# Two-layer decoder on one core: where the low parts of layer 0's weights are computed

## The chip, the core and the metric

The kernel runs on one core of one Trainium2 chip. A core has TensorE (PE, the matrix engine), VectorE (DVE), ScalarE (ACT), GpSimd (POOL) and SyncE (SP, which here only issues transfers). The metric is the device time of one execution in microseconds (us); the figure of a kernel is the median of its runs.

## The reference, cut to what matters

Two post-norm decoder layers over 512 tokens of width 1024, in float32. Layer 0 has two head groups, differential attention (4 heads) and a sparse attention (8 query heads in 2 groups, each with a compressed, a selected and a window branch); layer 1 has a forgetting attention with 16 heads. Each layer ends in a squared-ReLU MLP.

```python
for layer in range(DEPTH):                      # DEPTH = 2
    if layer % 2 == 0:
        h = x @ w_in_even[li]
        ...
        mix = jnp.concatenate([o_a, o_b], axis=-1) @ w_out_even[li]
    else:
        h = x @ w_in_odd[li]
        ...
    x = layer_norm(ALPHA * x + mix, ...)
    x = layer_norm(ALPHA * x + sqrelu_mlp(x, mlp_w_up[layer], mlp_w_down[layer]), ...)
```

## The kernel before, in words

**Split weights.** Every float32 operand of a large product is split into a high part (a rounded copy in the matrix engine's fp32r form, made by ScalarE) and a low part, `raw - high`. A product is three matmuls: high by high, high by low, low by high. Weights come in units of 128x1024: `unit` (L130 to L146) issues the transfer into `wraw` (2 buffers), ScalarE writes the high part (L144, into `whi`, 4 buffers) and a second engine writes the low part (L145, into `wlo`, 4 buffers):

```python
(eng or lo_engine[0]).tensor_tensor(lo[:, c], raw[:, c], hi[:, c].bitcast(F32), op=ALU.subtract)
```

Which engine that is stands in the one-element list `lo_engine`, VectorE at the start. The MLP's units (L387, L389) name VectorE themselves.

**Layer 0's attention.** A list written by hand, `EVEN_ORDER`, gives the pieces: W, B, Q, D and V are input projections (matmuls L180 to L182, each chunk of 256 columns needing two units), C is the compression, c0 and c1 are the compressed branch of groups 0 and 1, P are pairs of sparse heads and H are heads of the differential attention. A softmax of one head is a chain over the engines: scores on PE (L270, L271), the sum with the mask and its row minimum on DVE (L274), the exponential on ACT (L275), the reciprocal and the gate on DVE (L815, L816, or L852, L853, L856), the scaling of the first three row blocks on POOL (L321) and of the fourth on DVE (L323), transposes on PE (L288), and the split of the transposed blocks on ACT and DVE (L114, L116). A differential head joins its two softmaxes by four instructions on DVE (L859) and normalizes its output (L876 to L884, with a power on POOL, L881).

**Output projection and norm.** `out_proj` (L325, matmuls L335 to L337 and L357 to L359) takes eight units of `w_oe`, adds its results on DVE (L340, L361), and takes the first two units of the MLP's `w_up` into the tiles `sh` and `sl`, whose low part is also made by L145 on `lo_engine[0]`. The layer norm has a power on POOL (L212) and steps on DVE (L209 to L223).

**What sets the order.** The text is recorded and a scheduler places each engine's instructions. Each engine then runs its own list in order, and an instruction waits at the head of its engine until what it reads is written. SP issues the transfers in order; a transfer into `wraw` waits until both parts have been made from the buffer's last content.

**The lines of the change.** At piece c0 the loop sets `lo_engine` and `rope_engine` (the rotary embedding's engine) to GpSimd in one statement. Layer 1's attention sets `lo_engine[0] = G` once more at its start.

Of the kernel before, what the change touches and what calls it, by code (L numbers as in the profile page):

```python
# [60 lines left out]
def tile_trunk(ctx: ExitStack, tc: tile.TileContext, x, xt_in, ln_gain, ln_bias, w_up, w_down, w_ie, w_oe, lam_p, subln,  # L61
               pe, w1, b1, w2, w_io, f_bias, w_oo, consts, out):
    nc = tc.nc
    V, A, G, T = nc.vector, nc.scalar, nc.gpsimd, nc.tensor
# [63 lines left out]
    lo_engine, rope_engine = [V], [V]  # L128
# [460 lines left out]
    def even_layer():  # L589
        kbs = EVEN_KBS  # L590
        mh, ml = [None] * 8, [None] * 8
        for half in range(2):
            h, l = big(F32R), big(F32R)
            for i, kb in enumerate(kbs[4 * half:4 * half + 4]):
                mh[kb], ml[kb] = h[:, i], l[:, i]
        with ExitStack() as st:
            ap = pool("att0", st)
            even_attention(ap, mh, ml)
        return mh, ml, kbs, Weights(w_oe), x

    def even_attention(ap, mh, ml):
# [5 lines left out]
        def ahead():  # L607
            if len(todo) < len(widths):
                todo.append(wi.chunk(widths[len(todo)]))
# [39 lines left out]
        def windows():  # L649
            nats = {}  # L650

            def evac(bv, t0, n):
                tl = new(ap, "nat", [P, 2, 256], bufs=NB)
                A.activation(tl, bv, AF.Copy)
                for i in range(n):
                    nats[t0 + i] = (tl, i)
            gemm(evac)
            for tl, src in ((pet, pe), (b1t, b1), (w2t, w2)):
                nc.sync.dma_start(out=tl, in_=src)
            for j in range(2):  # L660
                b = transpose_nat(nats, 128 * j, "t")
                B = new(ap, "p", [P, 1280], bufs=2)[:, :1024].rearrange("p (l g n) -> p l g n", l=16, g=2)
                for g in range(2):
                    t2 = new(ap, "y", [P, 528], bufs=1)
                    G.memset(t2[:, 508:528], 0.0)
                    A.activation(t2[0:64, 0:512], b[64 * g:64 * g + 64, :], AF.Copy)
                    V.tensor_copy(t2[64:128, 0:511], b[64 * g:64 * g + 64, 1:512])
                    for h in range(2):
                        tv = t2[:, 16 * h:16 * h + 512].rearrange("p (n l c) -> p l n c", n=32, l=8)[:, :, :, 0]
                        G.tensor_tensor(B[:, 8 * h:8 * h + 8, g, :], tv,  # L670
                                        pet[:, j, 8 * h:8 * h + 8, None].to_broadcast([P, 8, 32]), op=ALU.add)
                Bs.append(B)
# [59 lines left out]
        def branch(br):  # L732
            nats = {}
            v = new(ap, "v", [P, NT, 2, 2, 64], F32R, bufs=4)

            def evac(bv, t0, n):
                tl = new(ap, "nat", [P, 2, 256], bufs=NB)
                A.activation(tl[:, :n, 0:128], bv[:, :, 0:128], AF.Copy)
                for g in range(2):
                    split(bv[:, :, 128 + 64 * g:192 + 64 * g], v[:, t0:t0 + n, g, 0, :], v[:, t0:t0 + n, g, 1, :])  # L740
                if br == 1:
                    A.activation(gate[:, t0:t0 + n], bv[:, :, 256:280], AF.Exp, scale=-1.0)
                rope_tok(ap, tl[:, :n, 0:128].rearrange("p n (h c) -> p n h c", h=2), t0, 2)
                for i in range(n):
                    nats[t0 + i] = (tl, i)
            gemm(evac)
            ks.append(stacks_k(ap, transpose_nat(nats, 0, "o" if br == 0 else "s"), "nk", KB))
            vs.append(v)
            if br == 1:
                gf = gate.rearrange("p a b -> p (a b)")  # L750
                V.tensor_scalar(gf, gf, 1.0, None, op0=ALU.add)
                V.reciprocal(gf, gf)
# [4 lines left out]
        def nsa_q(tag="g"):  # L757
            nats = {}

            def evac(bv, t0, n):  # L760
                tl = new(ap, "nat", [P, 2, 256], bufs=NB)
                A.activation(tl, bv, AF.Copy, scale=-SCALE)
                rope_tok(ap, tl.rearrange("p n (h c) -> p n h c", h=4), t0, 4)
                for i_ in range(n):
                    nats[t0 + i_] = (tl, i_)
            gemm(evac)
            qs = []
            for pr in range(2):
                qs += stacks_q(ap, transpose_nat(nats, 128 * pr, tag), 1.0)
            return qs  # L770
# [32 lines left out]
        def nsa_pair(g, pr, qs, pc):  # L803
            y = new(ap, "y", [P, SEQ], bufs=1)
            for e in range(2):
                h = 2 * pr + e
                o = bank("o")
                rows = slice(64 * pr, 64 * pr + 64)
                vc = vcb[rows, g, e].rearrange("p a c -> p (a c)")
                T.matmul(o, vc, pc[0][rows], start=True, stop=False)  # L810
                T.matmul(o, vc, pc[1][rows], start=False, stop=False)
                for br in range(2):
                    p, sm = softmax(ap, qs[h], ks[br][g])
                    r = new(ap, "rs", [P, 4], bufs=4)
                    V.reciprocal(r, sm[:, 4:8])  # L815
                    V.tensor_tensor(r, r, gv[:, :, 4 * g + h, 1 + br], op=ALU.mult)  # L816
                    scale_p(p, r)
                    pt = transpose_p(ap, p)
                    pv(o, pt, lambda j: vs[br][:, j, g].rearrange("p a c -> p (a c)"), False, br == 1)
                fold(ap, o, y, e)  # L820
            kb = 4 + 2 * g + pr
            split_y(y, mh[kb], ml[kb], V if kb == EVEN_KBS[-1] else G)


        def diff_qk(ta="g", tb="g"):
            nats = {}

            def evac(bv, t0, n):
                tl = new(ap, "nat", [P, 2, 256], bufs=NB)
                A.activation(tl[:, :, 0:128], bv[:, :, 0:128], AF.Copy, scale=-SCALE)  # L830
                A.activation(tl[:, :, 128:256], bv[:, :, 128:256], AF.Copy)
                rope_tok(ap, tl.rearrange("p n (h c) -> p n h c", h=4), t0, 4)
                for i_ in range(n):
                    nats[t0 + i_] = (tl, i_)
            gemm(evac)
            return stacks_q(ap, transpose_nat(nats, 0, ta), 1.0), stacks_k(ap, transpose_nat(nats, 128, tb), "nk", KB)

        def diff_v():
            v = [new(ap, "v", [P, 2, 2, 2, 128], F32R, bufs=4) for _ in range(2)]

            def evac(bv, t0, n):
                for h in range(2):
                    split(bv[:, :, h * 128:(h + 1) * 128], v[t0 // 2][:, :, h, 0, :], v[t0 // 2][:, :, h, 1, :])
            gemm(evac)
            return v
# [45 lines left out]
        got = {}  # L891
        for k in EVEN_ORDER:
            if k == "c0":
                lo_engine[0] = rope_engine[0] = G
            if k == "W":
                windows()
            elif k == "C":
                compress()
            elif k[0] == "B":
                branch(int(k[1]))  # L900
            elif k[0] == "Q":
                got[k] = nsa_q("o")
            elif k[0] == "D":
                got[k] = diff_qk(*['gg', 'og', 'tg', 'ts'][int(k[1])])
            elif k[0] == "V":
                got[k] = diff_v()
            elif k[0] == "H":
                h = int(k[1])
                diff_head(h, got.pop(f"D{h}"), got["V01" if h < 2 else "V23"], h % 2)
            elif k[0] == "c":  # L910
                got[k] = nsa_cmp(int(k[1]), got["Q" + k[1]])
            elif k[0] == "P":
                g = int(k[1])
                nsa_pair(g, int(k[2]), got[f"Q{g}"], got[f"c{g}"])
            if k in _EVEN:
                ahead()
# [218 lines left out]
```

## Time and profile before

| | us |
|---|---|
| median of 3 runs (1271.99 to 1275.66) | 1274.81 |
| the profiled execution, its own time | 1273.6 |
| its span in the trace | 1271.5 |
| PE busy in the span | 1237.5 (97%) |
| DVE busy | 878.2 (69%) |
| ACT busy | 647.3 (51%) |
| POOL busy | 301.2 (24%) |

The profiled execution took 2.1 us more than its span, and lies 1.2 us under the median. Matmuls are pipelined and their ends are modelled, so that a busy PE is not a PE at its peak. Layer 0's attention and output projection fill the span from some 30 to 330 us; piece c0 starts at about 80 us.

### The profile page before, as it was taken

To read this page: it belongs to the slowest core of one execution; us is meant where nothing else is said; L and a number is where in the kernel's file an instruction comes from. 1 tells how busy PE (TensorE), PEld (TensorE's weight loads), DVE (VectorE), ACT (ScalarE), POOL (GpSimd) and SP (SyncE) were. 2 spreads that over 40 slices of the span, in tenths; PEclk is the share of its full clock that TensorE was granted. 3 is DMA by queue.
4 is the path that set the end of the run, shared out by engine and by line. 5 is a ranking of instruction groups with operands and counts; after the bars stand their busy time and mean duration, and the time that the engine had idled before them with its cause. 6 is when DMAs were issued, how large, how long until landed. Compare 5 with 4: busy or idle time off the path is not lost.

```text
span 1271.5 us, 18398 instructions
## 1 busy us (share of the span) xinstructions
PE 1237.5 (97%) x7046; PEld 1079.2 (85%) x7046; DVE 878.2 (69%) x1602; ACT 647.3 (51%) x1185; POOL 301.2 (24%) x321
## 2 busy tenths in 40 slices
PE   7999998998999999999998999999999999999997
PEld 7999897898988888888887889889988888888886
DVE  5476768787859478495456788879767948669454
ACT  5266766764355454454423576767334445354530
POOL 1125565354200000000044354556510000000012
PEclk9999999999999999999999999999999999999999
DMA  7321121034414405234014322323630522505201
GB/s 274 114 87 54 34 67 35 5 129 138 167 61 132 133 25 175 67 96 146 17 50 150 101 84 92 92 88 129 231 112 23 182 84 68 164 34 159 73 17 50
DMA packets 46758, 125.15 MB, mean 98 GB/s; under 512 B 4672, under 2 KB 5184, under 8 KB 46672
## 3 DMA queue, kind: packets, MB, share of 16 engines
q1 hardware_dynamic: 46672, 123.99, 30.3%
q8 instruction: 55, 0.90, 0.3%
q14 instruction: 31, 0.25, 0.1%
HBM read 119.75 MB, written 4.23 MB: 98 GB/s over the span
## 4 chain that ended last, share of the span: by engine, by line
PE 86%; DVE 6%; DMA 3%; ACT 2%; issue 1%; POOL 1%; SPq 0%; DVEq 0%; ACTq 0%; POOLq 0%
PE g L193 11%; PE g L194 11%; PE g L195 11%; PE g L180 4%; PE g L181 4%; PE g L182 4%; PE s L478 3%; PE t L288 3%; PE s L479 3%; PE s L480 2%; DMA wraw<-w_up 2%; PE s L270 2%; PE o L480 2%; PE t L478 2%; PE o L478 2%; PE o L479 2%
## 5 line engine op out<-in xcount | busy, mean ns | idle before, releaser
L194 PE MATMUL g<-big,wlo 128*128 128x512 f32 x608 | 236.8, 391 | 0.0
L195 PE MATMUL g<-big,whi 128*128 128x512 f32 x608 | 236.6, 390 | 0.0
L193 PE MATMUL g<-big,whi 128*128 128x512 f32 x608 | 236.3, 390 | 0.0
L144 ACT ACTIVATE whi<-wraw 128x1024 fp32r<-128x1024 f32 (+3 forms) x120 | 125.3, 1045 | 112.5 <-DMA wraw<-w_up 37.1
L212 POOL TENSOR_TENSOR ve<-ve,nhalf 128x1 f32<-128x1 f32 x16 | 15.9, 991 | 647.0 <-DVE ve L211 647.0
L145 DVE TENSOR_TENSOR wlo<-wraw,whi 128x1024 fp32r<-128x1024 f32 (+2 forms) x69 | 84.3, 1228 | 96.5 <-ACT whi L144 96.4
L145 POOL TENSOR_TENSOR wlo<-wraw,whi 128x1024 fp32r<-128x1024 f32 (+2 forms) x51 | 123.4, 2425 | 94.6 <-ACT whi L144 82.3
L195 PEld LDWEIGHTS g<-big,whi 128*128 128x128 f32 x608 | 114.2, 188 | 23.6
L193 PEld LDWEIGHTS g<-big,whi 128*128 128x128 f32 x608 | 114.2, 188 | 23.2 <-issue 0.2
L194 PEld LDWEIGHTS g<-big,wlo 128*128 128x128 f32 x608 | 114.1, 188 | 23.1
L180 PE MATMUL g<-whi,big 128*128 128x256 f32 (+2 forms) x416 | 120.3, 289 | 0.6 <-DVE fz L946 0.4
L182 PE MATMUL g<-whi,big 128*128 128x256 f32 (+2 forms) x416 | 119.6, 287 | 0.0
L181 PE MATMUL g<-wlo,big 128*128 128x256 f32 (+2 forms) x416 | 119.1, 286 | 0.0
L414 DVE TENSOR_TENSOR wlo<-wdr,whi 128x1024 fp32r<-128x1024 f32 x72 | 87.4, 1218 | 44.4 <-ACT whi L413 44.4
L275 ACT ACTIVATE p<-p,sm 128x128 f32<-128x128 f32 (+3 forms) x160 | 89.2, 558 | 45.7 <-DVE sm L274 44.5
L395 ACT ACTIVATE big<-g 128x512 f32<-128x512 f32 x64 | 38.2, 597 | 134.4 <-PE g L195 134.4
L413 ACT ACTIVATE whi<-wdr 128x1024 fp32r<-128x1024 f32 x72 | 75.9, 1055 | 48.2 <-PE t L480 29.6
L321 POOL TENSOR_TENSOR p<-p,rs 128x128 f32<-128x128 f32 (+2 forms) x108 | 71.5, 688 | 93.2 <-DVE rs L970 40.4
L180 PEld LDWEIGHTS g<-whi,big 128*128 128x128 f32 x416 | 79.1, 190 | 2.2 <-ACT fv L114 0.6
L182 PEld LDWEIGHTS g<-whi,big 128*128 128x128 f32 x416 | 79.1, 190 | 0.7 <-issue 0.4
L181 PEld LDWEIGHTS g<-wlo,big 128*128 128x128 f32 x416 | 79.1, 190 | 0.6
L116 DVE TENSOR_TENSOR ptl<-t,pth 128x384 fp32r<-128x384 f32 (+1 forms) x108 | 63.1, 595 | 21.1 <-ACT pth L114 20.4
(313 smaller groups left out, 3093.0 us busy)
## 6 DMA issues: line engine op xcount, KB each, us to landing
wraw<-w_up SPq DMA_DIRECT2D x64, 512.0 KB, 3.7
wdr<-w_down SPq DMA_DIRECT2D x64, 512.0 KB, 4.7
wraw<-w_io SPq DMA_DIRECT2D x22, 512.0 KB, 3.3
wraw<-w_ie SPq DMA_DIRECT2D x18, 512.0 KB, 3.7
v<-w SPq DMA_DIRECT2D x8, 512.0 KB, 5.2
wraw<-w_oe SPq DMA_DIRECT2D x8, 512.0 KB, 3.6
cb<-c_dram SPq DMA_DIRECT2D x16, 256.0 KB, 3.2
wraw<-w_oo SPq DMA_DIRECT2D x8, 512.0 KB, 3.4
```

The lines of the kernel that those rows point to most:

```text
L144: A.activation(hi[:, c], raw[:, c], AF.Copy)
L145: (eng or lo_engine[0]).tensor_tensor(lo[:, c], raw[:, c], hi[:, c].bitcast(F32), op=ALU.subtract)
L180: T.matmul(bv[:, tt], xh, h, start=first, stop=False)
L181: T.matmul(bv[:, tt], xh, l, start=False, stop=False)
L182: T.matmul(bv[:, tt], xl, h, start=False, stop=last)
L193: T.matmul(b[:, a:e], h[:, cs], xh, start=k == 0, stop=False)
L194: T.matmul(b[:, a:e], l[:, cs], xh, start=False, stop=False)
L195: T.matmul(b[:, a:e], h[:, cs], xl, start=False, stop=k == 7)
L275: A.activation(pv, pv, AF.Exp, bias=sm[:, i:i + 1], scale=-1.0, accum_out=sm[:, 4 + i:5 + i])
L413: A.activation(hi, r, AF.Copy)
L414: V.tensor_tensor(lo, r, hi.bitcast(F32), op=ALU.subtract)
L478: T.matmul(bv, hh, us[m][0][:, k], start=first, stop=False, skip_group_check=True)
```

## The change

The one statement that set both engines now sets the rotary embedding's alone. So `lo_engine[0]` stays VectorE until layer 1 sets it to GpSimd.

```diff
             if k == "c0":
-                lo_engine[0] = rope_engine[0] = G
+                rope_engine[0] = G
```

On POOL 20 instructions of L145 are gone (18 that write `wlo`, 2 that write `sl`), and 20 more stand on DVE. The scheduler has also set the instructions of all five engines anew at places between c0 and the MLP's start; behind that all orders are as before. Three places:

On DVE, around the joining of head H0's two softmaxes (`p_2333` and `p_2311`; `wlo_3674` and `wlo_3734` are low parts of the first two units of the output projection). After the change:

```order
L274 ISA p_2311,sm_2312<-s_2328,K_68 128x512
L274 ISA sm_2312 128x1
L145 TENSOR_TENSOR wlo_3674<-wraw_3671,whi_3673 128x1024
L880 TENSOR_SCALAR ss_2241<-ss_2241 128x2
L783 TENSOR_TENSOR ft_2288<-s_2255,K_68 128x128 x4
...
L784 TENSOR_REDUCE pcm_2289<-ft_2288 128x16
L145 TENSOR_TENSOR wlo_3734<-wraw_3731,whi_3733 128x1024
L853 TENSOR_SCALAR rs_2355<-rs_2355,lam_137 128x4
```

Before the change the same stretch of DVE has no L145; both stood on POOL, one behind the other.

On DVE near the end of the attention, where the last head's first softmax (`p_3525`) is made; before:

```order
L274 ISA p_3525,sm_3526<-s_3532,K_68 128x256
L274 ISA sm_3526 128x1
L340 SCALAR_TENSOR_TENSOR big_3658<-big_3658,g_3797 128x256 x2
L274 ISA p_3525,sm_3526<-s_3537,K_68 128x384
L274 ISA sm_3526 128x1
L116 TENSOR_TENSOR ptl_3456<-t_3450,pth_3455 128x512
```

and after:

```order
L274 ISA p_3525,sm_3526<-s_3532,K_68 128x256
L274 ISA sm_3526 128x1
L145 TENSOR_TENSOR wlo_3930<-wraw_3927,whi_3929 128x1024
L116 TENSOR_TENSOR ptl_3456<-t_3450,pth_3455 128x512
L340 SCALAR_TENSOR_TENSOR big_3658<-big_3658,g_3857 128x256 x2
L116 TENSOR_TENSOR ptl_3464<-t_3459,pth_3463 128x384
L274 ISA p_3525,sm_3526<-s_3537,K_68 128x384
```

A low part now stands between two of this softmax's steps. In this stretch, from the unit `wlo_3918` on, there are four of them.

On SP, after the output projection, the difference in the issue of the MLP's first transfers (`wdr` are units of `w_down`, `wraw` units of `w_up`):

```order
 L405 DMA wdr_4589<-w_down 128x2x512
+L136 DMA wraw_4382<-w_up 128x1024
 L405 DMA wdr_4591<-w_down 128x2x512
+L136 DMA wraw_4388<-w_up 128x1024
 L405 DMA wdr_4593<-w_down 128x2x512
-L136 DMA wraw_4382<-w_up 128x1024
 L405 DMA wdr_4595<-w_down 128x2x512
-L136 DMA wraw_4388<-w_up 128x1024
```

The two units of `w_up` are issued two places earlier.

## Rows read from the trace of the kernel before

**Rows 1.** The page: the chain that ended last, its share by engine.
```profile
PE 86%; DVE 6%; DMA 3%; ACT 2%; issue 1%; POOL 1%; SPq 0%; DVEq 0%; ACTq 0%; POOLq 0%
```
**Rows 2.** Stretches of the span: length, each engine's busy us (x instructions), clock, DMA.
```profile
120.00:150.00 30.00, 28.13 (x201) 24.81 (x200) 23.30 (x69) 22.82 (x60) 17.22 (x26) 1.00 0.11 36
180.00:205.00 25.00, 22.59 (x181) 21.84 (x181) 18.44 (x52) 15.66 (x44) 18.54 (x26) 0.99 0.20 63
268.00:300.00 32.00, 29.61 (x224) 28.25 (x222) 27.22 (x67) 17.75 (x48) 14.72 (x11) 0.95 0.24 67
85.00:316.00 231.00, 219.09 (x1634) 203.35 (x1633) 171.48 (x460) 151.18 (x388) 122.50 (x176) 0.99 0.20 64
```
**Rows 3.** Waits of PE from 80 to 345 us: total us, times, longest.
```profile
PE t L288 <- DVE p L859: 2.5, 2, 2.3
PE g L357 <- DVE big L340: 2.1, 1, 2.1
...
PE g L193 <- ACT big L114: 1.0, 1, 1.0
```
**Rows 4.** Instructions of POOL from 85 to 316 us: busy us, mean ns, idle before.
```profile
L145 POOL TENSOR_TENSOR wlo<-wraw,whi 128x1024 fp32r<-128x1024 f32 x18 | 44.2, 2462 | 22.2 <-ACT whi L144 16.5 <-issue 5.7
```
**Rows 5.** The page: all instructions of L321, busy us, mean ns, idle before.
```profile
L321 POOL TENSOR_TENSOR p<-p,rs 128x128 f32<-128x128 f32 (+2 forms) x108 | 71.5, 688 | 93.2 <-DVE rs L970 40.4
```
**Rows 6.** Line 145 on DVE: shortest, median and longest ns.
```profile
L145 DVE TENSOR_TENSOR wlo<-wraw,whi x69: 736/1225/1782, 26.4 to 1199.2; 128x1024 fp32r<-128x1024 f32 x66, 128x840 fp32r<-128x840 f32 x2, 128x560 fp32r<-128x560 f32 x1
```
**Rows 7.** DVE in order of time: start us, length us, instruction.
```profile
109.60 2.29 DVE L816 TENSOR_TENSOR rs<-rs,gate 128x4 f32<-128x4 f32 x1
...
120.51 0.17 DVE L816 TENSOR_TENSOR rs<-rs,gate 128x4 f32<-128x4 f32 x1
...
166.51 0.23 DVE L853 TENSOR_SCALAR rs<-rs,lam 128x4 f32<-128x4 f32 x1
...
198.85 4.03 DVE L859 SCALAR_TENSOR_TENSOR p<-p,rs,p 128x128 f32<-128x128 f32 x4
...
275.37 4.09 DVE L859 SCALAR_TENSOR_TENSOR p<-p,rs,p 128x128 f32<-128x128 f32 x4
...
284.50 1.58 DVE L853 TENSOR_SCALAR rs<-rs,lam 128x4 f32<-128x4 f32 x1
...
291.68 1.94 DVE L859 SCALAR_TENSOR_TENSOR p<-p,rs,p 128x128 f32<-128x128 f32 x4
...
293.86 1.98 DVE L880 TENSOR_SCALAR ss<-ss 128x2 f32<-128x2 f32 x1
...
301.27 0.17 DVE L880 TENSOR_SCALAR ss<-ss 128x2 f32<-128x2 f32 x1
...
311.08 2.00 DVE L222 SCALAR_TENSOR_TENSOR big<-big,mv,lng 128x512 f32<-128x512 f32 x1
...
324.09 0.74 DVE L222 SCALAR_TENSOR_TENSOR big<-big,mv,lng 128x512 f32<-128x512 f32 x1
```
**Rows 8.** POOL in order of time, L145 alone: start us, length us, idle before.
```profile
107.11 4.76 POOL L145 TENSOR_TENSOR wlo<-wraw,whi 128x1024 fp32r<-128x1024 f32 x2 [1.06 <-ACT whi L144]
...
199.56 5.57 POOL L145 TENSOR_TENSOR wlo<-wraw,whi 128x1024 fp32r<-128x1024 f32 x2 [2.14 <-ACT whi L144]
...
275.54 2.44 POOL L145 TENSOR_TENSOR wlo<-wraw,whi 128x1024 fp32r<-128x1024 f32 x1 [0.56 <-ACT whi L144]
283.66 2.39 POOL L145 TENSOR_TENSOR wlo<-wraw,whi 128x1024 fp32r<-128x1024 f32 x1 [5.67 <-issue]
...
293.04 2.78 POOL L145 TENSOR_TENSOR wlo<-wraw,whi 128x1024 fp32r<-128x1024 f32 x1 [3.72 <-ACT whi L144]
...
307.77 4.76 POOL L145 TENSOR_TENSOR sl<-wraw,sh 128x1024 fp32r<-128x1024 f32 x2 [2.75 <-ACT sh L144]
```
**Rows 9.** The chain that ended last, around the output projection's end: start us, us.
```profile
315.78 12.31 DMA wraw<-w_up
328.11 1.06 ACT whi L144
```

## The prediction

> **What bounds the kernel now.** I read the chain that ended last first: 86% of it is PE, 6% DVE and 1% POOL [rows 1]. So an engine's work counts only where PE stands for it. The change touches layer 0 from piece c0 to the first MLP transfers, 85 to 316 us. Over that stretch PE is busy 219.09 of 231 us, DVE 171.48 (74%), ACT 151.18, POOL 122.50 [rows 2]; the rest of the program keeps its order. The reader should see next that PE's 12 us of idle time are not spread evenly: 1.87 us fall in 120 to 150, 2.41 in 180 to 205 and 2.39 in 268 to 300 [rows 2], and the longest waits there end on DVE: the joining of a head's two softmaxes (L859) for 2.3 us, an output-projection add (L340) for 2.1 us [rows 3]. Elsewhere PE has input projections to fill in with.
>
> Then I looked at what DVE does at those places. Four joining instructions take 1.94 us together at 291.68, but 4.03 at 198.85 and 4.09 at 275.37 [rows 7]. Just then POOL runs low parts, two from 199.56 for 5.57 us and one from 275.54 for 2.44 us [rows 8]. The same holds for tiny instructions: L816 takes 2.29 us at 109.60 and 0.17 at 120.51, L853 1.58 at 284.50 and 0.23 at 166.51, L880 1.98 at 293.86 and 0.17 at 301.27, and in the norm L222 takes 2.00 at 311.08 and 0.74 at 324.09 [rows 7]. Each of the long ones lies under a low part on POOL, and those of 109.60 and 284.50 end with it [rows 8]. An instruction of DVE that reads only SBUF is held up until POOL's instruction is over; those that read PSUM in the same stretches keep their length. That is the main thing to price.
>
> **What the change removes.** 18 low parts of 2462 ns (44.2 us) [rows 4] and the two into `sl` (4.76 us) [rows 8] leave POOL, 49.0 us in all; PE waits for none of them directly [rows 3]. What they give back is DVE's stalls. At the three heads' ends: 4.03 - 1.94 = 2.09, 4.09 - 1.94 = 2.15, 1.58 - 0.23 = 1.35, 1.98 - 0.17 = 1.81, together 7.4 us [rows 7]. These stand where PE runs dry, and I count them in full. The stall of 2.29 - 0.17 = 2.12 us at 109.60 lies under projections; the softmax behind it is late all the same, and the projections that cover it are then missing later, so I count half, 1.0 us (bounds 0 and 2.1). The norm's 2.00 - 0.74 = 1.26 us comes below.
>
> **What it adds.** 20 low parts on DVE at its median of 1225 ns [rows 6]: 24.5 us. The order shows where. Six stand in the two stretches of the joined heads: two ahead of the first joining, four among the last head's steps. They are 6 x 1.225 = 7.35 us. DVE idles 25.00 - 18.44 = 6.56 us in the one and 32.00 - 27.22 = 4.78 in the other [rows 2], so between nothing and all of it fits; the scheduler places them between steps that wait for ACT or PE, and I take half, 3.7 us. Of the other fourteen, twelve lie where PE has projections ready; I cost them at nothing. With that cover gone they, and the two into `sl`, cost 14 x 1.225 = 17.15 us. What waits behind a low part on DVE is a step of a softmax, and for that PE's transposes.
>
> **The remaining contention.** POOL keeps 122.50 - 44.2 - 4.8 = 73.5 us of work, a share of 0.32 [rows 2, 4, 8], mostly L321 with a mean of 688 ns [rows 5]. A low part on DVE reads two SBUF tiles, so it can be held up as L816 was. An estimate from these rows: 20 x 0.32 x half of 0.688 = 2.2 us; a third of it on the path, 0.7 us. The longest low part on DVE took 1782 ns [rows 6], 0.56 over the median, so nothing is so far as long as the stalls that go. The Trainium skill, on the page "SBUF — State Buffer", section "Who interferes with whom", states that a DVE instruction with both inputs in SBUF contends with a GpSimd instruction that reads SBUF, whichever starts first holding the shared ports to its end. By that rule the moved instruction keeps the quarrel and only changes sides: POOL's scaling (L321) would now stand behind a low part of 1.2 us, as DVE's steps stood behind one of 2.4. The trace agrees with the direction in which DVE waits, and the sum by the rule would be some 2 us worse than mine.
>
> **The norm and the first MLP units.** The two low parts into `sl` now stand on DVE just ahead of the norm's first adds: 2 x 1.225 = 2.45 us more, less the stall of 1.26: 1.2 us. Against it, the transfer of `w_up` issued at 315.78 landed after 12.31 us, ACT made its high part at 328.11, and the transposed rows' copy stood behind that [rows 9]; PE waited 1.0 us for it [rows 3]. The two transfers are now issued two places earlier, so I take that wait as gone. Net 0.2 us (bounds -1.0 and 1.2).
>
> **The new order on PE.** Projections move ahead of some attention steps in 120 to 150. PE idles 1.87 us there [rows 2]; I take half of it as saved, 0.9 us (bounds 0 and 1.9).
>
> **The sum.** -7.4 - 1.0 + 3.7 + 0.7 + 0.2 - 0.9 = -4.7 us. The profiled execution took 1273.6 us, 1.2 under the median of the runs: 1268.9, which against the median is 1270.1. I say 1270.
>
> **The rivals.** *An even trade.* If nothing covers the six low parts, DVE pays 7.35 us for 7.4, and the rest of the sum is -1.0 us. In favour: in 268 to 300 DVE is busy 85% of the time with a stall counted in [rows 2], and the order puts a low part inside the last head's softmax itself. Against: the stall hits L859 and L880, which PE waits for, while the scheduler can move a low part to where DVE waits. The time is 1271 to 1278, say 1274.
>
> *DVE becomes the bound, slower.* DVE's load rises to 171.5 - 10.8 + 24.5 + 2.2 = 187.4 of 231 us, 81%, while POOL falls to 73.5. If half of the fourteen stand on the path as well: 8.6 + 7.35 + 2.2 - 10.8 = +7.3 us, 1282; all of them would make it 1291. It decides from nine low parts on the path on (9 x 1.225 = 11.0, against 10.8 of stalls). For it: the attention's steps need DVE between PE's, and low parts come in pairs. Against: PE is short of work in only a few of these stretches. The skill's page "Perfetto Trace Analysis", section "Optimizing Scalar/DVE Operations", would move work off a saturated DVE even to GpSimd, while warning that the shared port may eat the gain. At 74% this trace doesn't show a saturated DVE over the whole stretch.
>
> *The whole of it comes back.* Low parts all covered, both stalls and the idle time in full: -7.4 - 2.1 - 1.9 - 1.0 = -12.4 us, 1262.
>
> That the change does nothing is excluded: the order shows all twenty moved.
>
> **Chances and range.** About 0.3%, 3.8 us, is what a measurement of this kernel can tell from no change. Forecast (faster, its own range 1265 to 1271) 0.40; all of it back 0.05; even trade 0.33; DVE the bound 0.22. So faster 0.45, same 0.33, slower 0.22. The range reaches from just above the best case to just under the slower rival's time, 1263 to 1281; some 2 in 10 stay outside, most of it above.
>
> **What would show it.** In the changed kernel's trace the joinings (L859) should all take about 2 us for four, and L816, L853 and L880 no more than some 0.8 us. L145 on DVE should stay near 1.2 us in the mean. POOL's busy time should fall by 49 us, DVE's rise by some 14 to 16. PE's idle time at 198 to 203 and 292 to 296 should shrink. The forecast is wrong if PE's longest waits go to steps that stand behind an L145 on DVE (L274 or L116 releasing PE late), or if the stretch without projections, after 205 us, begins sooner and lasts longer by as much, since then DVE sets the attention's pace wherever the low parts stand.

## The result, and the profile after

The changed kernel takes 1285.67 us (median of 4 runs, 1283.98 to 1286.05) against 1275.24 beside it: the ratio is 1.0084 (95% interval 1.0063 to 1.0104), so by the ratio it is **slower by 10.7 us** where I had forecast 4.7 us less. One execution each of two kernels further down, 1575.77 and 2126.77 us at mean granted clocks of 0.73 and 0.65, is left out of their figures. The profiled span is 1284.2 us, 12.7 more than before. On the page POOL's busy time falls from 301.2 to 257.6 us and DVE's rises from 878.2 to 888.3.

The stretches of [rows 2] in the changed kernel (length, busy us of PE, weight loads, DVE, ACT, POOL, granted clock, DMA):

```profile
120.00:150.00 30.00, 27.95 (x200) 25.06 (x199) 21.54 (x61) 19.62 (x52) 12.42 (x27) 1.00 0.11 37
180.00:205.00 25.00, 19.95 (x162) 19.08 (x162) 17.40 (x47) 12.96 (x37) 7.04 (x15) 0.96 0.19 65
268.00:300.00 32.00, 31.45 (x255) 30.63 (x253) 26.81 (x70) 18.71 (x49) 7.90 (x11) 1.00 0.20 68
85.00:316.00 231.00, 212.82 (x1559) 196.41 (x1558) 171.81 (x464) 147.66 (x384) 76.85 (x154) 0.96 0.16 53
```

PE is idle for 18.2 us of the 231 in the place of 11.9, and its granted clock is 0.96 in the place of 0.99. DVE is no busier over the stretch than before, and in 180 to 205 us it idles 7.6 of 25 us, so over these stretches no saturated DVE is to be seen. Only from 200 to 205 us, where PE waits longest, is it busy throughout (5.00 us); before the change it was nearly so there (4.86 us). PE's waits from 80 to 345 us (total us, times, longest):

```profile
PE s L270 <- DVE sm L274: 7.1, 5, 2.8
PE t L887 <- DVE ft L884: 2.4, 2, 1.5
PE s L270 <- DVE ft L783: 1.2, 1, 1.2
...
PE t L288 <- DVE ptl L116: 1.1, 3, 0.4
PE t L288 <- POOL p L321: 1.1, 3, 0.6
```

The two long waits of [rows 3] are gone (L859 and L340); in their place PE's scores wait for DVE's masked sums (L274), a wait that before was 0.2 us long. Where the time goes can be dated by instructions that both programs have: the first head's last transposes (L887 into `o`), the last head's (L887 into `t`), and the first product of the MLP with full tiles (L193). In the kernel before (count, shortest, median and longest ns, first and last start):

```profile
L887 PE MATMUL o<-ident,ft x12: 270/286/435, 189.3 to 299.6; 128*128 128x128 f32 x12
L887 PE MATMUL t<-ident,ft x4: 271/300/328, 305.0 to 305.7; 128*128 128x128 f32 x4
L193 PE MATMUL g<-big,whi x48: 389/389/446, 344.9 to 377.0; 128*128 128x512 f32 x48
```

and in the changed one:

```profile
L887 PE MATMUL o<-ident,ft x12: 270/314/472, 196.5 to 302.3; 128*128 128x128 f32 x12
L887 PE MATMUL t<-ident,ft x4: 403/460/476, 312.2 to 314.1; 128*128 128x128 f32 x4
L193 PE MATMUL g<-big,whi x48: 387/389/444, 356.5 to 388.6; 128*128 128x512 f32 x48
```

The changed program's transposes at the start (L623) begin 0.9 us earlier (20.4 against 21.3), so the delays are 196.5 - 189.3 + 0.9 = 8.1 us at the first head, 312.2 - 305.0 + 0.9 = 8.1 at the last, and 356.5 - 344.9 + 0.9 = 12.5 at the MLP. **Two losses**, then: 8 us before some 200 us, and 4.4 us between the attention's end and the MLP. Behind that it is 1.1 us more (1284.2 - 356.5 = 927.7 against 1271.5 - 344.9 = 926.6). PE's four longest idle times of the early one (start, length, what it waited for):

```profile
198.89 0.39 PE L270 MATMUL s<-nka,q 128*128 128x256 f32 x1 [1.23 <-DVE ft L783]
201.89 0.50 PE L270 MATMUL s<-nka,q 128*128 128x512 f32 x1 [1.87 <-DVE sm L274]
204.76 0.58 PE L270 MATMUL s<-nka,q 128*128 128x256 f32 x1 [1.95 <-DVE sm L274]
208.39 0.69 PE L270 MATMUL s<-nka,q 128*128 128x384 f32 x1 [2.83 <-DVE sm L274]
```

and DVE there:

```profile
196.75 1.23 DVE L145 TENSOR_TENSOR wlo<-wraw,whi 128x1024 fp32r<-128x1024 f32 x1 [0.21 <-ACT whi L144]
197.89 0.16 DVE L880 TENSOR_SCALAR ss<-ss 128x2 f32<-128x2 f32 x1
197.96 0.88 DVE L783 TENSOR_TENSOR ft<-s,K 128x128 f32<-128x128 f32 x4
...
200.15 1.22 DVE L145 TENSOR_TENSOR wlo<-wraw,whi 128x1024 fp32r<-128x1024 f32 x1
201.28 0.22 DVE L853 TENSOR_SCALAR rs<-rs,lam 128x4 f32<-128x4 f32 x1
201.41 0.42 DVE L274 CUSTOM_DVE_ANT_0 p<-s,K 128x256 f32<-128x256 f32 x1
```

Two readings fit these rows. By the first (A) it is the order: the scheduler, told of another engine, has arranged layer 0 anew, and six tiles of input projections (`g_335` to `g_587`) now stand in the mean 21 to 56 attention instructions earlier on PE, so that they are used up when the heads' ends need cover. By the second (B) it is DVE's load: the two low parts above stand ahead of the very steps that PE waits for.

### The profile page after: what moved, and what is told of

Read it like the earlier page. It is cut to its first block, busy times and chain, and to the rows that moved or that the text cites. A ratio compares the mean times of both kernels' runs of the same rounds, so it can differ in the third digit from the quotient of the medians.

```text
span 1284.2 us, 18403 instructions
## 1 busy us (share of the span) xinstructions
PE 1243.4 (97%) x7046; PEld 1083.7 (84%) x7046; DVE 888.3 (69%) x1622; ACT 647.1 (50%) x1185; POOL 257.6 (20%) x301
## 4 chain that ended last, share of the span: by engine, by line
PE 87%; DVE 6%; ACT 3%; DMA 2%; issue 1%; POOL 1%; DVEq 0%; SPq 0%; ACTq 0%; POOLq 0%
PE g L193 11%; PE g L194 11%; PE g L195 11%; PE g L180 4%; PE g L181 4%; PE g L182 4%; PE t L288 3%; PE s L478 3%; PE s L479 3%; PE s L480 2%; PE t L478 2%; PE o L478 2%; PE o L480 2%; PE o L479 2%; PE s L270 2%; PE t L479 2%
## 5 line engine op out<-in xcount | busy, mean ns | idle before, releaser
L193 PE MATMUL g<-big,whi 128*128 128x512 f32 x608 | 236.4, 391 | 0.0
L145 DVE TENSOR_TENSOR wlo<-wraw,whi 128x1024 fp32r<-128x1024 f32 (+2 forms) x87 | 106.6, 1230 | 109.0 <-ACT whi L144 108.6
L193 PEld LDWEIGHTS g<-big,whi 128*128 128x128 f32 x608 | 114.3, 188 | 23.5 <-issue 0.4
L321 POOL TENSOR_TENSOR p<-p,rs 128x128 f32<-128x128 f32 (+2 forms) x108 | 71.5, 688 | 130.6 <-DVE rs L816 55.4
L145 POOL TENSOR_TENSOR wlo<-wraw,whi 128x1024 fp32r<-128x1024 f32 (+2 forms) x33 | 79.5, 2415 | 72.6 <-ACT whi L144 65.9
L116 DVE TENSOR_TENSOR ptl<-t,pth 128x384 fp32r<-128x384 f32 (+1 forms) x108 | 63.3, 596 | 17.3 <-ACT pth L114 16.6
```

The source lines that it names most:

```text
L193: T.matmul(b[:, a:e], h[:, cs], xh, start=k == 0, stop=False)
```

## The experiments

**Engine and order apart.** The programs' instructions have the same names, so one program can be made to issue in the order of the other. A table of names is added, and a dependency without a wait from each instruction to the one ahead of it:

```diff
-        tile_trunk(tc, *args)
+        tile_trunk(tc, *args); keep_order(tc, nc, ORDER)
...
+        for prev, i in zip(line, line[1:]):
+            tc.add_manual_dep(i, prev.name, mybir.DependencyInfo(
+                mybir.DependencyClass.NoSync, mybir.DependencyReason.DATA), reason="keep_order")
```

The changed kernel with the table of before on all five engines:

> All twenty low parts on VectorE as in the changed kernel, but every engine issues layer 0 in the order of the kernel before; the low parts alone are put in where the scheduler finds room on VectorE (eight of them between two steps of a softmax). Theory A, the loss is the new order of projections and attention steps that the scheduler chose: the time falls to that of the kernel before or under it, 1264 to 1275 us, with the four stalls of L859, L853 and L880 gone. Theory B, the loss is VectorE's load itself (a low part of 1.23 us stands ahead of steps that TensorE waits for): it stays at 1280 us or more.

The kernel before with the table of the changed one:

> The kernel before, low parts on GpSimd, but every engine issues layer 0 in the order of the changed kernel. Theory A: as slow as the changed kernel or slower, 1283 to 1292 us, since it has the order and still has GpSimd's stalls of VectorE. Theory B: the load is off VectorE, so 1270 to 1277 us, as the kernel before.

| ratio to the kernel before | its order | the changed kernel's order |
|---|---|---|
| low parts on POOL | 1 | 1.0126 (1.0113 to 1.0139), 1290.33 us |
| low parts on DVE | 0.9985 (0.9973 to 0.9997), 1272.32 us | 1.0084 (1.0063 to 1.0104), 1285.67 us |

The engine makes 1.9 us less in the one order and 5.4 less in the other. The order makes 16.1 us more with the low parts on POOL and 12.6 with them on DVE. B falls: the slowest of the four has no low part on DVE at all. So **the order is the loss**, whichever engine makes the low parts. No run holds a kernel to its own order; that the added dependencies cost nothing is argued from their having no wait, and not measured.

**By halves of the change.** Ten of the twenty low parts each, with the scheduler free: `lo_engine[0] = G` behind the attention's loop, or the kernel before with `lo_engine[0] = V` there.

> The changed kernel with the ten low parts of the output projection and of the first unit of w_up put back on GpSimd (the ten of the input projections stay on VectorE). In the changed kernel's trace some 8 us are lost before 205 us and some 5 at the start of the norm and the MLP. If the ten late low parts make the 5, the time is 1279 to 1282 us and the first MLP product starts at about 335 us; if the new order or the load in the first part makes all of it, 1284 to 1287 us.

> The other half: the ten low parts of the input projections on GpSimd as before, those of the output projection and of the first unit of w_up on VectorE. If the two losses add, 1278 to 1281 us (5 us over the kernel before, all of them after 300 us); if the late ten cost nothing by themselves, 1272 to 1276 us.

1286.76 us (ratio 1.0097, 1.0084 to 1.0110) and 1278.88 (1.0028, 1.0019 to 1.0038). The first is telling: half of the change undone brings nothing back. The second kernel has the input projections up to `g_587` exactly where the kernel before has them, and is 4.5 us late at the MLP: the second loss alone.

**Projections held back.** The changed kernel, with PE's matmuls of the named tiles tied behind the attention instruction that they followed before:

```diff
+        for i in own[at:at + int(count)]:
+            tc.add_manual_dep(i, "I-" + prev, ... NoSync ...)
```

> The changed kernel with one thing of the order undone: TensorE may issue the matmuls of three chunks of input projections (six tiles, from the tile g_335 to g_587) no earlier among the attention's steps than the kernel before did; in the changed kernel they stand 21 to 56 attention instructions earlier in the mean. Everything else is the scheduler's. Theory A1, these projections are spent too early, and are missing as cover behind 197 us: 1276 to 1280 us (some 8 of the 10 us lost are back). Rival A2, it is some other part of the new order (the order of the attention's own steps, or of ScalarE and VectorE): 1283 us or more.

> The changed kernel with the output projection's matmuls (both passes) held back in the same way, the input projections free. In the changed kernel its tiles stand up to 24 attention instructions earlier, and the norm starts with TensorE dry. Theory A1: the 3 to 5 us lost behind 300 us come back, 1280 to 1283 us. Rival: the norm's loss comes from the order of the transfers and of GpSimd's L212, which this leaves as they are: 1284 to 1287 us.

1285.73 us (1.0089, 1.0071 to 1.0107) and 1284.24 (1.0079, 1.0061 to 1.0097). **A1 fell in this form.** With the input projections held:

```profile
120.00:150.00 30.00, 25.85 (x174) 21.89 (x173) 25.23 (x69) 22.37 (x58) 13.30 (x23) 1.00 0.11 36
195.00:210.00 15.00, 13.15 (x101) 12.02 (x100) 13.12 (x40) 9.17 (x22) 5.99 (x13) 1.00 0.10 30
```

PE is busy 13.15 of 15 us at 195 to 210, where the changed kernel has 7.12 (below), but it now loses 4.15 us in 120 to 150, in the place of 2.05. The tie was one-sided: the scheduler put five of the six tiles 2 to 11 attention instructions *later* than the kernel before. So the loss moved to where the projections were taken from; that they are spent too early is shown as far as this, that holding them back moves the loss, and not that it cures it. Holding the output projection brought the MLP's start 4.1 us forward (353.2 - 21.2 = 332.0 from the first L623, against 336.1). The runs show less of it: three lie at 1282.1 to 1282.7 and three at 1285.8 to 1287.7. The profiled one, of the upper group, has waits in layer 1 between 700 and 800 us (L270 for L274, 3.5 us in all in the place of 0.4); the edit also names layer 1's output projection, but that starts only at 873 us, and where these waits come from stays open.

The second loss can be read from the 10 us behind the last head's transposes into `t`. Before the change:

```profile
305.00:315.00 10.00, 9.01 (x69) 8.14 (x68) 7.95 (x14) 2.93 (x4) 5.75 (x4) 1.00 0.84 231
```

in the changed kernel, and with the output projection held back:

```profile
312.00:322.00 10.00, 7.15 (x29) 6.15 (x30) 7.60 (x15) 2.88 (x7) 1.22 (x2) 0.52 0.66 208
...
312.00:322.00 10.00, 8.32 (x63) 7.38 (x62) 7.94 (x14) 2.49 (x3) 0.70 (x2) 1.00 0.78 218
```

With its output projection issued early (these tiles stand up to 24 attention instructions ahead of their old places), the changed kernel's PE waits 1.5 and 0.9 us for L884 at these transposes and does 29 matmuls in these 10 us in the place of 69, at a granted clock of 0.52 in the place of 1.00. An estimate from the row, 0.48 x 7.15 = 3.4 us, makes most of the 4.4 us slow work and not waiting. With the projection held back the clock stays at 1.00.

**Early and late.** The order of before on all engines up to the first softmax of pair P10 (203 us), or from there on:

> The changed kernel with the order of the kernel before on every engine up to the first softmax of group 1's first pair (about 203 us), and the scheduler's order behind it, where TensorE's projections stand as in the changed kernel. If the two losses are separate, the early one is gone and the late one stays: 1276 to 1280 us, with TensorE's loss at 195 to 210 us back to some 5 us and that at 300 to 330 us still some 9 us or more. If the early order makes all of it, 1271 to 1275 us.

> The reverse: the scheduler's own order up to about 203 us, with its projections 21 to 56 attention instructions early, and the order of the kernel before on every engine behind it. If the two losses are separate: 1278 to 1282 us, with the loss at 195 to 210 us still near 10 us and that at 300 to 330 us back to some 5. If the late order makes all of it, 1271 to 1275 us.

1281.45 us (1.0062, 1.0050 to 1.0074) and 1278.61 (1.0038, 1.0025 to 1.0051). Against the 0.9985 with the whole order of before, the scheduler's late order costs 9.8 us and the early one 6.8; together 16.6, where both at once cost 12.6. Neither makes all of it, and the early order's time lies above what I had expected of either case.

**Engine by engine.** The order of before on some engines, the rest free:

> The changed kernel with TensorE's instructions alone in the order of the kernel before; ScalarE, VectorE, GpSimd and the transfers as the scheduler puts them. Holding back the input projections alone had moved the loss (from 195 to 210 us to 135 to 150 us) and not removed it, so if TensorE's order as a whole carries the loss: 1271 to 1275 us. If the order of VectorE's and ScalarE's steps has a share of its own: 1277 us or more.

> The changed kernel with TensorE's and VectorE's order of the kernel before; ScalarE, GpSimd and the transfers as the scheduler puts them. With TensorE's order alone it took 1282 us. If VectorE's order carries the other half: 1270 to 1274 us. If ScalarE's, GpSimd's or the transfers' order carries it: 1279 us or more.

> The counterpart: the order of the kernel before on every engine but VectorE, whose order is the scheduler's. If VectorE's order carries the other half: 1279 to 1283 us, as with TensorE's order alone. If the others carry it: 1270 to 1274 us.

> VectorE alone in the order of the kernel before; the scheduler then puts six of the eight early projection tiles back to within 2 attention instructions of their old place by itself, and those of D2 (g_583) 16 too early. If VectorE's order is what decides, and TensorE's only follows it: 1271 to 1276 us. If TensorE's order has to be right as well: 1278 us or more.

> The changed kernel with TensorE's and ScalarE's order of the kernel before; VectorE, GpSimd and the transfers as the scheduler puts them. If the high part ahead of the exponential on ScalarE is what TensorE's order lacked: 1273 to 1276 us, without TensorE's wait of 1.7 us at 264 us. If GpSimd's order or that of the transfers is: 1280 us or more.

> The counterpart: TensorE's, GpSimd's and the transfers' order of the kernel before, ScalarE and VectorE as the scheduler puts them, the high part again ahead of the exponential. If ScalarE's order is what is missing: 1280 to 1283 us. If GpSimd's or the transfers' is: 1273 to 1276 us.

| in the order of before | us | ratio |
|---|---|---|
| none (the changed kernel) | 1285.67 | 1.0084 |
| DVE | 1290.91 | 1.0130 (1.0117 to 1.0143) |
| PE | 1280.47 | 1.0067 (1.0051 to 1.0083) |
| PE, POOL, transfers | 1283.25 | 1.0076 (1.0063 to 1.0090) |
| PE, DVE | 1277.08 | 1.0030 (1.0018 to 1.0041) |
| PE, ACT | 1276.43 | 1.0022 (1.0013 to 1.0031) |
| PE, ACT, POOL, transfers | 1274.37 | 1.0005 (0.9991 to 1.0018) |
| all | 1272.32 | 0.9985 (0.9973 to 0.9997) |

Neither PE's order alone nor DVE's holds the loss; those of ACT, POOL and the transfers were not run alone, and PE with DVE came out between what I had expected of either case. PE's alone ends the early loss but for 1.6 us (the first head ends 190.9 - 21.3 = 169.6 us after the first L623, against 168.0 before and 176.1 after), and then PE waits at another place:

```profile
264.39 0.33 PE L288 MATMUL t<-ident,p 128*128 128x128 f32 x1 [1.70 <-POOL p L321]
265.15 0.34 PE L288 MATMUL t<-ident,p 128*128 128x128 f32 x1 [0.43 <-POOL p L321]
265.94 0.69 PE L288 MATMUL t<-ident,p 128*128 128x128 f32 x2 [0.45 <-POOL p L321]
```

In the same kernel ACT has put a weight's high part ahead of the last exponential of that softmax:

```profile
259.76 1.06 ACT L144 ACTIVATE whi<-wraw 128x1024 fp32r<-128x1024 f32 x1
260.71 0.72 ACT L275 ACTIVATE p<-p,sm 128x512 f32<-128x512 f32 x1
```

and DVE a low part of 1.23 us (260.86) ahead of its reciprocal. With PE and ACT both in the old order that wait is gone and, by the ratios, 5.7 us with it; with PE, POOL and the transfers it stays, 1.70 us long. So PE's and ACT's order together bring back 7.9 of the 12.6 us. PE's and DVE's bring back 6.9, so the shares of the engines don't add up. DVE's order alone makes it worse than none; why it does, no run takes apart.

**Price and place of the low parts, order held.** Beside the whole order of before: four low parts moved in DVE's own list, or eighteen made short (256 of 1024 columns, so that the kernel computes other values).

```diff
-L145 wlo_3674, L145 wlo_3734          (behind the join L859)
+L145 wlo_3674 ahead of L116 ptl_2909, L145 wlo_3734 ahead of L116 ptl_2917
-L145 sl, L361, L145 sl, L361
+L361, L361, L145 sl, L145 sl
```

> All low parts on VectorE in the order of the kernel before, as in the run of that order, with four low parts at other places of VectorE's own order: the pair behind the join at 201 us goes 40 us back, to where VectorE waits for ScalarE (1.26 and 2.29 us at 242 and 245 us), and the two into sl behind the two adds L361 that TensorE waits for. If only the place of a low part decides, TensorE's wait of 2.15 us at 204 us and 0.6 of the 0.9 us at 309 us go: 1269 to 1271 us. If VectorE has no room at all, the wait turns up behind: 1272 to 1274 us.

```diff
+            few = eng is pl is None and lo_engine[0] is V and rope_engine[0] is G; q = slice(0, w) if few else c; ...
```

> The same order with the eighteen low parts into wlo a quarter as wide (256 of 1024 columns; the rest of the weights' low parts is taken from these columns, so the values change): VectorE does some 15 us less, in the same order on every engine. If the five low parts that stand in the chain of that run are what VectorE's load costs (three of them shortened here), 1269 to 1270 us; if the whole load is on the path, 1257 to 1259 us; if it is all covered, 1272 us.

1268.30 us (0.9955, 0.9941 to 0.9969) and 1268.42 (0.9949, 0.9935 to 0.9963). With the order alone restored PE still waits for the pair, 2.35 us long on DVE right behind the join:

```profile
201.52 2.35 DVE L145 TENSOR_TENSOR wlo<-wraw,whi 128x1024 fp32r<-128x1024 f32 x2
203.79 0.28 DVE L274 CUSTOM_DVE_ANT_0 p<-s,K 128x128 f32<-128x128 f32 x1
```

```profile
204.13 0.56 PE L270 MATMUL s<-nka,q 128*128 128x384 f32 x1 [2.15 <-DVE sm L274]
```

With the pair moved L274 follows the join at once, at 200.88, and PE's wait for L274 falls from 2.3 us in all to the 0.2 of before:

```profile
198.79 1.94 DVE L859 SCALAR_TENSOR_TENSOR p<-p,rs,p 128x128 f32<-128x128 f32 x4
200.88 0.29 DVE L274 CUSTOM_DVE_ANT_0 p<-s,K 128x128 f32<-128x128 f32 x1
```

Moving four low parts is worth as much as shortening eighteen: these took 424 ns in the median, 18 x (1.226 - 0.424) = 14.4 us of DVE's work, and gave 3.9 us by the medians (by the ratios 4.6, with an estimated interval of 2.2 to 6.9). The moved version beats both kernels, by 0.45% and by 1.3%.

**The same move on POOL.** The kernel before in its own order, only the pair of 199.56 us [rows 8] 40 us later in POOL's list:

> The kernel before, low parts on GpSimd and every engine in its order, with only the pair of low parts of 199.56 us put 40 us later on GpSimd's queue, to where VectorE mostly waits. If place decides and not the engine: the join L859 at 199 us takes 1.94 in the place of 4.03 us, TensorE's wait for it (2.3 us) goes, and the time is 1271 to 1273 us. If the join's length was hidden anyway, as before, 1274 us.

1270.42 us (0.9971, 0.9960 to 0.9983): the join takes 1.94 us there too, with no engine changed.

## Why the prediction was wrong, point by point

**The step that failed is "The new order on PE".** It priced the new order at -0.9 us, from PE's 1.87 us of idle time in 120 to 150 us, "bounds 0 and 1.9". I read a difference on every engine over 230 us as one local gain, bounded it by the idle time of one stretch, and took all other waits from a trace made in the old order. Measured it is +12.6 us. No bound of mine could hold that: projections taken early are missing later, and that price stands where they are missing. What I had named as the sign of error, a stretch without projections that "begins sooner and lasts longer", is what the trace shows; but I had tied it to DVE's load, and the kernel with the same order and no low part on DVE has it too. My other sign came true too, as PE's longest waits went to L274 and the one of 201.89 stands right behind a low part, but that kernel has waits for L274 as well:

```profile
PE s L270 <- DVE sm L274: 5.8, 6, 2.8
```

**The stalls given back: mechanism right, size half.** In the changed kernel no joining takes more than 1.21 us alone, L853 at most 0.23, L880 0.17, L816 0.39, as foretold. But the 7.4 us "in full" were not all on PE's path. With the order held, PE's waits for L859 fall from 2.5 to 0.4 us and those for L340 from 2.1 to 0.3 [rows 3]:

```profile
PE s L270 <- DVE sm L274: 2.3, 2, 2.2
PE t L288 <- DVE ptl L116: 2.0, 4, 0.8
...
PE g L357 <- DVE big L361: 0.9, 1, 0.9
...
PE t L288 <- DVE p L859: 0.4, 2, 0.2
...
PE g L357 <- DVE big L340: 0.3, 1, 0.3
```

That is 3.9 us; that the rest had other work over it is inferred from there being no such wait.

**The low parts on DVE: about right in size.** I took 3.7 us for six of them and 1.2 for the two into `sl`. With the order held PE's waits grow by 2.1 us for L274 (0.2 before; the pair), 0.6 for L116 (1.4 before) and 0.6 for L361 (0.3 before): 3.3 us. From the short ones, 3.9 us for 14.4 us of work, about a quarter of the load is on the path, some five low parts of the twenty, where the slower rival needed nine; by the ratios' interval it is three to ten, so that rival's count isn't excluded by this run.

**Remaining contention: there, and on the other side.** POOL fell by 43.6 us, not 49.0, and small steps of it are now held up. Engine by engine, DVE's low part and POOL's rotary step beside it in the changed kernel:

```profile
129.69 1.27 DVE L145 TENSOR_TENSOR wlo<-wraw,whi 128x1024 fp32r<-128x1024 f32 x1 [0.46 <-ACT whi L144]
```

```profile
129.83 1.24 POOL L576 TENSOR_TENSOR rp<-nat,K 128x32 f32<-128x32 f32 x1
```

A step of 0.25 us in the median takes 1.24 and ends with the low part. The rule of the Trainium skill cited ahead ("SBUF — State Buffer", "Who interferes with whom") says just this, and the trace agrees. On PE it is the 1.1 us for L321 in the waits above; I had 0.7. My reading that any instruction of DVE on SBUF alone is held up was too wide. This reciprocal, in the kernel before, kept its 0.18 us under the low part of 283.66:

```profile
284.29 0.18 DVE L852 RECIPROCAL rs<-sm 128x4 f32<-128x4 f32 x1 [0.22 <-ACT p L275]
```

**The norm.** I took PE's wait of 1.0 us behind the `w_up` transfer as gone and 0.2 us in all. A wait of 0.7 us is left there, and the attention's end to the MLP takes 4.4 us longer, most of it at the lower clock as shown above. Holding the output projection back gave 4.1 of 12.5 us at the MLP's start; which of its tiles it is, and what the order of the transfers adds, stays open.

**Without the order's step** my sum is -3.8 us. The kernel in the old order came out at -1.9 (-3.4 to -0.4): half of my sum, the stalls being the over-sized term (3.9 of 7.4 us). It lies nearer to the rival of an even trade (-1.0), and the traces themselves show that trade: up to the first product of the MLP the profiled executions take 323.6 us (before) and 345.1 - 21.4 = 323.7 (order held) from the first L623, so the 1.9 us rests on the medians. The outcome lies among my rivals' times (1282 to 1291) by another cause than theirs.

## What to carry to other kernels

When a scheduler places the instructions, moving an operation to another engine is two changes, and the one that isn't in the diff can be the larger. Compare the orders over the whole stretch first, and if they differ, price that as an unknown of either sign; pinning the new program to the old order (and the old to the new) separates the two in two runs. An operation that nobody waits for soon is best judged by its place in the queue: a pair of low parts put 40 us back gained 3.4 us on POOL without any change of engine, where the change of engine in the old order gained 1.9.

## What the runs showed of the hardware that was not expected

A wait of PE costs more than its length when it lets the clock fall. The moved pair on POOL took 4.03 - 1.94 = 2.09 us from the join and gave 3.4 us (1273.79 to 1270.42; by the ratio's interval 2.2 to 5.1). PE in 195 to 210 us, in the kernel before:

```profile
195.00:210.00 15.00, 12.59 (x85) 11.88 (x84) 12.15 (x34) 9.73 (x28) 8.67 (x11) 0.89 0.23 72
```

with the pair moved on POOL:

```profile
195.00:210.00 15.00, 13.65 (x97) 11.81 (x95) 12.58 (x45) 12.64 (x38) 5.17 (x11) 1.00 0.01 2
```

and in the changed kernel:

```profile
195.00:210.00 15.00, 7.12 (x39) 5.86 (x39) 13.31 (x41) 8.40 (x23) 4.32 (x5) 0.77 0.21 72
```

Before, the granted clock is 0.89 in the mean, so that PE stood at the lower of its two levels (1.2 GHz) for part of it, after 2.3 us of waiting; an estimate from the row is 0.11 x 15 = 1.65 us at most. In the changed kernel, with 7.9 us of waits, it is 0.77. The last head's four transposes, 300 ns in the median before, took 460 ns there, just behind another wait, and the 10 us from there ran at 0.52 as shown above. So part of the 12.6 us is not waiting at all but work at half the speed behind it.
